# Phase tables by summed turns and one sine, and reciprocal roots as a power on GpSimd, in a two-block sequence kernel

## The chip, the cores and the metric

One core of one Trainium2 chip runs the whole program. The metric is the device time in microseconds of one execution; the kernel before was run three times.

## The reference

The input is one sequence of 256 tokens of width 1024 and a context of 256 tokens. The first block has two layers. Each normalizes tokens and context, multiplies by a wide input matrix, and feeds three branches: latent attention, multi-scale pooling and a gated linear attention (GLA) in four heads, run forwards and backwards. The branches are merged under gates and multiplied by an output matrix, and the result is normalized and added to the residual. The second block has a delta-rule recurrence (RWKV-7), a diagonal state-space branch (S5) with 32 groups of 64 states, a merge, and a convolutional feed-forward part. Cut to what the change touches:

```
def rmsnorm(x, g):
    y = x * lax.rsqrt(mean(x * x, -1) + 1e-6)
    return y * g

def s5_branch(u, a_re, a_im, ...):
    lam = complex(a_re, a_im);  dt = exp(log_step)[:, None]
    a_bar = exp(lam * dt)
    b_bar = ((a_bar - 1.0) / lam)[..., None] * complex(b_re, b_im)
    states = associative_scan(s5_combine, (a_bar at each token, bu))
    y = real(einsum('gcp,blgp->blgc', c, states)) + d * ug
```

The kernel runs the state-space recurrence with the real factor |a_bar| alone and turns the phases outside of it. For that it needs the cosine and the sine of t times the angle for all 256 tokens t and each of the 2048 states: 16 tables of 128 states by 512 columns (256 cosines, 256 sines).

## The kernel before

Activations lie transposed, features in the partitions and tokens in the columns. Weights come in units of 128x2048 as two tiles `raw` (seven buffers), issued on SyncE's queue (L409, L417). `split` (L419 to L428) cuts each into a high part `wh`, cast by ScalarE (L424), and a low part `wl`, subtracted by VectorE or GpSimd (L426); four buffers each. `mm3` (L441) runs three matmuls per weight tile. The order on each engine is made by a scheduler from the order in the program and the readiness of operands; an operation that stands late in the program can be placed early where its engine is free.

**Reciprocal roots.** Column sums of squares come out of TensorE as one column per 128 tokens (`token_sums`, L460), so a root is taken of a tile of 128x2, 128x4 or 128x16. `rsqrt` (L482 to L497) does it on VectorE: an integer guess (L488), then two refinement steps, nine instructions in one chain up to L496. `bcast` (L468) spreads the result over the partitions by transposes. `rstd` and `rstd_cols` (L471 to L480) serve the latent attention and the GLA heads. `boundary` (L540 to L567) serves the passage from one residual to the next normed input: a root `r` of the mean square of the branch output, four steps (L562 to L565) that make the mean square of the new residual from sums that are ready beforehand, a second root, and two broadcasts. `enter` (L657 to L668) then goes through the eight tiles of the residual: `update_x` adds the normed output on GpSimd (L649, L650) or on VectorE (L653, L654), and `build_h` (L634 to L640) makes the normed input. The updates on VectorE are held behind the second root (`issue_after(b.chain_end.ins)`).

**Phase tables.** `s5_prepare` (L1351 on) works out the angle in turns, splits t into 16 a + c and takes 32 sines and 32 cosines for each state (L1376 to L1389). Then each of 16 tables is made of them by the addition theorem on GpSimd: four products, a difference and a sum of 128x256 (L1443 to L1448), and a DMA on SyncE's queue writes it to DRAM (L1450). The tables are read back in the second block (L1568). This runs woven with the merge of the GLA branch in layer 0 (`weave(s5_prepare(b), 19, merge(2, ygla), 8)`), and for this stretch `lo_every` is set so that all weight splits go to VectorE:

```
        b.lo_every = 1 << 30
        weave(s5_prepare(b), 19, merge(2, ygla), 8)
        b.lo_every = 4
```

The merge takes a tanh of each gate (ScalarE, L939), a product (VectorE, L943) and a sum (VectorE, L947).

Of the kernel before, what the change touches and what calls it, by code (L numbers as in the profile page):

```python
# [10 lines left out]
F32 = mybir.dt.float32  # L11
# [3 lines left out]
AF = mybir.ActivationFunctionType  # L15
ALU = mybir.AluOpType
AX = mybir.AxisListType.X

P = 128
# [66 lines left out]
def _constants():  # L86
    c = Layout()
# [22 lines left out]
    sg[:64, 3], sg[64:, 3] = 0.0, 1 / TAU  # L110
    c.add("sgn", sg)
    c.add("iota", np.broadcast_to(np.concatenate([16.0 * np.arange(16), np.arange(16)]).astype(np.float32), (P, 32)))
    c.add("zero", np.zeros((P, 1), np.float32))
    c.add("one", np.ones((P, P), np.float32))
    c.add("mean", np.full((P, 1), 1.0 / D, np.float32))
    c.add("mean2", np.full((P, 1), 2.0 / D, np.float32))
    j = np.arange(P)
    masks = []
    i = j[:, None] // 64 * 64 + np.arange(64)
# [239 lines left out]
class B:  # L359
# [119 lines left out]
        n = self.token_sums(ps, 0, acc)  # L479
        return self.bcast(self.rstd_cols(ps[:, :n], n, dim), n, pool)  # L480

    def rsqrt(self, m, n):  # L482

        nc = self.nc
        r = self.sm.tile([P, 16], F32, tag="r", name="r")[:, :n]
        t = self.sm.tile([P, 16], F32, tag="t", name="t")[:, :n]
        u = self.sm.tile([P, 16], F32, tag="u", name="u")[:, :n]
        nc.vector.tensor_scalar(r.bitcast(I32), m.bitcast(I32), -0.5, 1597463007.0, ALU.mult, ALU.add)  # L488
        nc.vector.tensor_mul(t, r, r)
        nc.vector.tensor_mul(t, t, m)  # L490
        nc.vector.scalar_tensor_tensor(r, t, -3.0, r, ALU.add, ALU.mult)
        nc.vector.tensor_mul(t, r, r)  # L492
        nc.vector.tensor_mul(t, t, m)
        nc.vector.tensor_scalar(u, t, -0.375 / 32, 1.25 / 8, ALU.mult, ALU.add)  # L494
        nc.vector.tensor_mul(u, u, t)
        self.chain_end = nc.vector.scalar_tensor_tensor(r, u, -0.9375, r, ALU.add, ALU.mult)  # L496
        return r  # L497


# [144 lines left out]
def update_x(b, k, st, xs, s_, pr, rs, on_pool):  # L644

    nc = b.nc
    o_ = st["out"][k]
    if on_pool:
        nc.gpsimd.tensor_mul(o_.ap, o_.ap, rs.ap)  # L649
        nc.gpsimd.tensor_add(xs[s_][k], xs[s_][k], o_.ap)  # L650
    else:
        with b.tc.issue_after(b.chain_end.ins):
            nc.vector.tensor_mul(o_.ap, o_.ap, pr[:, 0:256])  # L653
            nc.vector.tensor_add(xs[s_][k], xs[s_][k], o_.ap)  # L654
    b.S.drop(o_)


# [13 lines left out]
def trunk(b, l, xs, st, A):  # L671

    nc, S = b.nc, b.S
# [21 lines left out]
    if st is None:  # L695
# [3 lines left out]
        for s_ in range(2):  # L699
            acc, t = S.cols(256), S.cols(256)  # L700
# [5 lines left out]
            S.drop(acc, t)  # L706
        A = b.sm.tile([P, 16], F32, tag="bA", name="bA")[:, :4]
        nc.vector.tensor_scalar(A, ps[:, :4], EPS, None, ALU.add)
        pr2 = b.bcast(b.rsqrt(A, 4), 4, b.pb)
    if st:  # L710
        first_units()
    shift, G = b.mod[l][0], b.mod[l][1]
# [11 lines left out]
    else:  # L724
        h, st = st
        xpart = enter(b, st, xs, 1, A[:, 2:4], lambda k: [t[:, XC] for t in h[k]], gain_, shift_, (0, 1, 3, 5, 7))
        A = next(xpart)
# [597 lines left out]
MAGIC = 12582912.0  # L1325
# [25 lines left out]
def s5_prepare(b):  # L1351
# [26 lines left out]
    nc.vector.tensor_sub(m, m, r)  # L1378
    nc.vector.tensor_tensor(r3, iob, fl.unsqueeze(2).broadcast_to((P, N, 32)), ALU.mult)
    nc.vector.tensor_add(m, m, r)  # L1380
    sn, cs = S.get(), S.get()
    for t, ph in ((sn, 0.0), (cs, 0.25)):
        if ph:
            nc.vector.tensor_scalar(m, m, ph, None, ALU.add)
        nc.vector.tensor_scalar(r, m, MAGIC, -MAGIC, ALU.add, ALU.add)
        nc.vector.tensor_sub(t, m, r)
    zero = b.after((sn, cs), 0.0)
    for t in (sn, cs):
        nc.scalar.activation(t, t, AF.Sin, bias=zero, scale=6.283184)  # L1389
    S.put(m, r)  # L1390
    yield
    sn3, cs3 = (t.rearrange("p (a c) -> p a c", c=32) for t in (sn, cs))

    s1, c1 = sn3[:, :, 17], cs3[:, :, 17]
    ur, ui, n2, kr, ki = sm("ur"), sm("ui"), sm("n2"), sm("kr"), sm("ki")
    nc.vector.tensor_mul(ur, rho, c1)
    nc.vector.tensor_scalar(ur, ur, -1.0, None, ALU.add)
# [34 lines left out]
        b.s5["w"].append(d)  # L1432
    S.put(cre, cren, cimn)
    yield
    ring = [(S.get(), S.get()) for _ in range(2)]
    for i in range(16):
        tab, tp = ring[i % 2]
        a3 = lambda t: t.rearrange("p (a c) -> p a c", c=16)
        can = cs[:, i * 32:i * 32 + 16].unsqueeze(2).broadcast_to((P, 16, 16))
        san = sn[:, i * 32:i * 32 + 16].unsqueeze(2).broadcast_to((P, 16, 16))  # L1440
        cbn = cs[:, i * 32 + 16:i * 32 + 32].unsqueeze(1).broadcast_to((P, 16, 16))
        sbn = sn[:, i * 32 + 16:i * 32 + 32].unsqueeze(1).broadcast_to((P, 16, 16))
        nc.gpsimd.tensor_tensor(a3(tab[:, 0:256]), can, cbn, ALU.mult)  # L1443
        nc.gpsimd.tensor_tensor(a3(tp[:, 0:256]), san, sbn, ALU.mult)
        nc.gpsimd.tensor_tensor(a3(tab[:, 256:512]), san, cbn, ALU.mult)
        nc.gpsimd.tensor_tensor(a3(tp[:, 256:512]), can, sbn, ALU.mult)
        nc.gpsimd.tensor_sub(tab[:, 0:256], tab[:, 0:256], tp[:, 0:256])
        nc.gpsimd.tensor_add(tab[:, 256:512], tab[:, 256:512], tp[:, 256:512])  # L1448
        d = b.tc.dram_tile([P, 512], F32, name=f"s5t{i}")
        nc.sync.dma_start(d, tab)  # L1450
        b.s5["tab"].append(d)
        yield
    S.put(sn, cs, *ring[0], *ring[1])


def second_block(b, xs, st, A):
# [172 lines left out]
    def rwkv_chain():  # L1629
# [29 lines left out]

        m16 = b.sm.tile([P, 16], F32, tag="m16", name="m16")  # L1660
        nc.vector.tensor_scalar(m16, nk[:, 0:16], 1e-24, None, ALU.max)
        rn = b.rsqrt(m16, 16)
        rnk = b.sm.tile([P, 16], F32, tag="rnk", name="rnk")
        nc.vector.tensor_copy(rnk, rn)
        yield
# [225 lines left out]
            S.drop(sq)  # L1891
        m16 = b.sm.tile([P, 16], F32, tag="m16", name="m16b")
        nc.vector.tensor_scalar(m16, nk[:, 0:16], 1.0 / 64, 64e-5, ALU.mult, ALU.add)
        rn = b.rsqrt(m16, 16)
        rnk = b.sm.tile([P, 16], F32, tag="rnk", name="rnk2")
        nc.vector.tensor_copy(rnk, rn)
        for q in range(4):
# [211 lines left out]
```

## Time and profile before

| | |
|---|---|
| median of 3 runs | 1556.37 us (1552.61 to 1558.96) |
| the profiled execution | 1556.99 us |
| its span, first to last instruction | 1555.2 us |
| mean granted TensorE clock | 0.954 |
| VectorE, ScalarE, GpSimd busy | 1101.0, 688.8, 491.1 us |

The span is the time between the first and the last instruction of the trace. Busy is the union of an engine's instructions. Idle time stands in front of the instruction that ended it, with what released it. Not every idle time costs something: only one on the engine that sets the end does.

### The profile page before, as it was taken

To read this page: it belongs to the slowest core of one execution; us is meant where nothing else is said; L and a number is where in the kernel's file an instruction comes from. 1 tells how busy PE (TensorE), PEld (TensorE's weight loads), DVE (VectorE), ACT (ScalarE), POOL (GpSimd) and SP (SyncE) were. 2 spreads that over 40 slices of the span, in tenths; PEclk is the share of its full clock that TensorE was granted. 3 is DMA by queue.
4 is the path that set the end of the run, shared out by engine and by line. 5 is a ranking of instruction groups with operands and counts; after the bars stand their busy time and mean duration, and the time that the engine had idled before them with its cause. 6 is when DMAs were issued, how large, how long until landed. Compare 5 with 4: busy or idle time off the path is not lost. (4 is left out here: it accounts for less than half of the span.)

```text
span 1555.2 us, 27544 instructions
## 1 busy us (share of the span) xinstructions
PE 1435.6 (92%) x10700; PEld 1216.2 (78%) x10700; DVE 1101.0 (71%) x2215; ACT 688.8 (44%) x1279; POOL 491.1 (32%) x503
## 2 busy tenths in 40 slices
PE   5999999998999999899998889979899999699996
PEld 1676776876788878886877789968668999699996
DVE  4565567887779555865579977768988549798843
ACT  3434445443433334454554455633532435376642
POOL 1000003354336954510035331334543003421212
PEclk8999999999999999899989999979999999799998
DMA  9534431321224253334024236734231325266560
GB/s 355 192 106 155 127 128 33 94 66 55 67 88 124 82 209 103 96 109 163 14 82 122 77 115 177 258 127 129 78 95 37 95 64 169 69 196 185 177 189 28
DMA packets 61043, 187.92 MB, mean 121 GB/s; under 512 B 7024, under 2 KB 8560, under 8 KB 60912
## 3 DMA queue, kind: packets, MB, share of 16 engines
q1 hardware_dynamic: 60912, 186.16, 38.2%
q8 instruction: 84, 1.38, 0.4%
q14 instruction: 47, 0.39, 0.1%
HBM read 180.10 MB, written 6.03 MB: 120 GB/s over the span
## 5 line engine op out<-in xcount | busy, mean ns | idle before, releaser
L424 ACT CAST wh<-raw 128x1024 fp32r<-128x1024 f32 (+1 forms) x296 | 279.5, 949 | 281.0 <-PE y L441 55.7
L426 DVE TENSOR_TENSOR wl<-raw,wh 128x1024 fp32r<-128x1024 f32 (+1 forms) x225 | 266.2, 1185 | 170.0 <-ACT wh L424 166.6
L426 POOL TENSOR_TENSOR wl<-raw,wh 128x1024 fp32r<-128x1024 f32 (+1 forms) x71 | 144.7, 2038 | 616.1 <-ACT wh L424 584.1
L441 PE MATMUL z_merge<-s,wh 128*128 128x512 f32 (+1 forms) x768 | 200.6, 351 | 1.8 <-ACT s L939 1.8
L441 PEld LDWEIGHTS z_merge<-s,wh 128*128 128x128 f32 x768 | 136.1, 198 | 19.7 <-ACT s L939 2.4
L441 PE MATMUL z_merge<-s,wl 128*128 128x512 f32 (+1 forms) x384 | 133.6, 348 | 0.3 <-DVE wl L426 0.2
L441 PE MATMUL pbr<-s,wh 128*128 128x256 f32 (+1 forms) x512 | 120.1, 326 | 0.8 <-DVE s L432 0.7
L441 PE MATMUL pup<-s,wh 128*128 128x256 f32 x656 | 118.5, 283 | 0.1
L441 PEld LDWEIGHTS pup<-s,wh 128*128 128x128 f32 x656 | 102.5, 192 | 0.2 <-ACT wh L424 0.2
L441 PE MATMUL y<-s,wh 128*128 128x256 f32 x496 | 98.1, 294 | 0.0
L441 PE MATMUL pwo<-s,wh 128*128 128x256 f32 (+1 forms) x448 | 94.1, 307 | 3.8 <-ACT s L1247 3.1
L441 PEld LDWEIGHTS pbr<-s,wh 128*128 128x128 f32 x512 | 86.8, 192 | 9.8 <-DVE s L432 1.0
L441 PE MATMUL pup<-s,wl 128*128 128x256 f32 x328 | 92.8, 283 | 0.0
L441 PEld LDWEIGHTS y<-s,wh 128*128 128x128 f32 x496 | 78.6, 193 | 7.8 <-issue 4.8
L441 PEld LDWEIGHTS z_merge<-s,wl 128*128 128x128 f32 x384 | 76.1, 198 | 9.5 <-DVE wl L426 1.1
L441 PE MATMUL pbr<-s,wl 128*128 128x256 f32 (+1 forms) x256 | 83.1, 325 | 0.0
L441 PEld LDWEIGHTS pwo<-s,wh 128*128 128x128 f32 x448 | 75.0, 199 | 7.7 <-ACT s L1247 3.7
L1134 ACT ACTIVATE s<-s 128x512 f32<-128x512 f32 (+1 forms) x64 | 33.2, 523 | 89.9 <-DVE s L1133 75.2
L441 PE MATMUL y<-s,wl 128*128 128x256 f32 x248 | 71.3, 287 | 0.0
L441 PE MATMUL pwo<-s,wl 128*128 128x256 f32 (+1 forms) x224 | 68.4, 306 | 1.5 <-DVE wl L426 1.5
L431 ACT CAST s<-s 128x256 fp32r<-128x256 f32 (+1 forms) x88 | 42.6, 488 | 60.7 <-DVE s L1204 17.9
L441 PE MATMUL pdn<-s,wh 128*128 128x256 f32 x352 | 63.4, 283 | 0.0
(480 smaller groups left out, 3618.8 us busy)
## 6 DMA issues: line engine op xcount, KB each, us to landing
raw<-wts SPq DMA_DIRECT2D x294, 512.0 KB, 4.4
s<-wts SPq DMA_DIRECT2D x57, 256.0 KB, 5.4
s5t<-s SPq DMA_DIRECT2D x16, 256.0 KB, 2.0
s<-s5t SPq DMA_DIRECT2D x16, 256.0 KB, 3.2
s<-xc SPq DMA_DIRECT2D x8, 256.0 KB, 5.0
x<-xc SPq DMA_DIRECT2D x8, 256.0 KB, 5.1
s<-tabs SPq DMA_DIRECT2D x4, 256.0 KB, 4.5
out<-s SPq DMA_DIRECT2D x8, 128.0 KB, 1.8
```

Of the source, the lines that this page charges most:

```text
L424: self.nc.scalar.copy(hi[:, :n], src)
L426: self.last_lo = eng.tensor_sub(lo[:, :n], src, hi[:, :n])
L431: self.nc.scalar.copy(hi, src)
L441: self.nc.tensor.matmul(ps, u, v[:, cols], start=start and n == 0, stop=stop and n == last)
L1134: nc.scalar.activation(E[:, lo:], E[:, lo:], AF.Exp, scale=1.0 / TAU)
```

## The change

The tables: the 32 small sines and cosines are no longer taken. VectorE adds the turns of 16 a and of c for all 256 tokens (once for the sine, once with a quarter turn more for the cosine), takes off the nearest whole number (two steps), and ScalarE takes one sine of the 512 columns. Four tables form a group: a helper (`after`, L445 on) waits for all four and hands a zero to the four sines, whose table set differs from that of the tanh. Of the small values only the step of one token is still needed (`s1`, `c1`).

The roots: `rsqrt` becomes a single power with exponent -0.5 on GpSimd, except for the first norm and the two 128x16 tiles, which keep the steps (`steps=True`). `chain_end` is now the power, so the hold moves from the updates on VectorE to those on GpSimd.

```
+    c.add("mhalf", np.full((P, 16), -0.5, np.float32))
...
-    def rsqrt(self, m, n):
+    def rsqrt(self, m, n, steps=False):
...
+        if not steps:
+            self.chain_end = nc.gpsimd.tensor_tensor(r, m, self.c("mhalf")[:, :n], ALU.pow)
+            return r
...
     if on_pool:
-        nc.gpsimd.tensor_mul(o_.ap, o_.ap, rs.ap)
-        nc.gpsimd.tensor_add(xs[s_][k], xs[s_][k], o_.ap)
+        with b.tc.issue_after(b.chain_end.ins):
+            nc.gpsimd.tensor_mul(o_.ap, o_.ap, rs.ap)
+            nc.gpsimd.tensor_add(xs[s_][k], xs[s_][k], o_.ap)
     else:
-        with b.tc.issue_after(b.chain_end.ins):
-            nc.vector.tensor_mul(o_.ap, o_.ap, pr[:, 0:256])
-            nc.vector.tensor_add(xs[s_][k], xs[s_][k], o_.ap)
+        nc.vector.tensor_mul(o_.ap, o_.ap, pr[:, 0:256])
+        nc.vector.tensor_add(xs[s_][k], xs[s_][k], o_.ap)
...
-    sn, cs = S.get(), S.get()
-    for t, ph in ((sn, 0.0), (cs, 0.25)):
-        if ph:
-            nc.vector.tensor_scalar(m, m, ph, None, ALU.add)
-        nc.vector.tensor_scalar(r, m, MAGIC, -MAGIC, ALU.add, ALU.add)
-        nc.vector.tensor_sub(t, m, r)
-    zero = b.after((sn, cs), 0.0)
-    for t in (sn, cs):
+    nc.vector.tensor_scalar(r, m, MAGIC, -MAGIC, ALU.add, ALU.add)
+    nc.vector.tensor_sub(m, m, r)
...
+    nc.vector.tensor_copy(s1, m3[:, :, 17])
+    nc.vector.tensor_scalar(c1, s1, 0.25, None, ALU.add)
+    nc.vector.tensor_scalar(k, c1, MAGIC, -MAGIC, ALU.add, ALU.add)
+    nc.vector.tensor_sub(c1, c1, k)
+    zero = b.after((s1, c1), 0.0)
+    for t in (s1, c1):
         nc.scalar.activation(t, t, AF.Sin, bias=zero, scale=6.283184)
...
+    nc.vector.tensor_copy(mc[:, 0:256].rearrange("p (i a) -> p i a", a=16), m3[:, :, 0:16])
+    nc.vector.tensor_scalar(mc[:, 256:512].rearrange("p (i a) -> p i a", a=16), m3[:, :, 0:16], 0.25, None, ALU.add)
+    rd = S.get()
     for i in range(16):
-        tab, tp = ring[i % 2]
...
-        nc.gpsimd.tensor_tensor(a3(tab[:, 0:256]), can, cbn, ALU.mult)
-        nc.gpsimd.tensor_tensor(a3(tp[:, 0:256]), san, sbn, ALU.mult)
-        nc.gpsimd.tensor_tensor(a3(tab[:, 256:512]), san, cbn, ALU.mult)
-        nc.gpsimd.tensor_tensor(a3(tp[:, 256:512]), can, sbn, ALU.mult)
-        nc.gpsimd.tensor_sub(tab[:, 0:256], tab[:, 0:256], tp[:, 0:256])
-        nc.gpsimd.tensor_add(tab[:, 256:512], tab[:, 256:512], tp[:, 256:512])
-        d = b.tc.dram_tile([P, 512], F32, name=f"s5t{i}")
-        nc.sync.dma_start(d, tab)
+        if i % 4 == 0:
+            tabs = [S.get() for _ in range(4)]
+        tab = tabs[i % 4]
+        t4 = tab.rearrange("p (e a c) -> p e a c", e=2, c=16)
+        for e in range(2):
+            am = mc[:, 256 * (1 - e) + 16 * i:256 * (1 - e) + 16 * i + 16].unsqueeze(2).broadcast_to((P, 16, 16))
+            bm = m3[:, i, 16:32].unsqueeze(1).broadcast_to((P, 16, 16))
+            nc.vector.tensor_tensor(t4[:, e], am, bm, ALU.add)
+        nc.vector.tensor_scalar(rd, tab, MAGIC, -MAGIC, ALU.add, ALU.add)
+        nc.vector.tensor_sub(tab, tab, rd)
+        if i % 4 == 3:
+            zero = b.after(tabs, 0.0)
+            for j, t in enumerate(tabs):
+                nc.scalar.activation(t, t, AF.Sin, bias=zero, scale=6.283184)
+                d = b.tc.dram_tile([P, 512], F32, name=f"s5t{i - 3 + j}")
+                nc.sync.dma_start(d, t)
```

## Rows read from the trace of the kernel before

**Rows 1.** The page's first part: busy us, share of the span, instructions.
```profile
PE 1435.6 (92%) x10700; PEld 1216.2 (78%) x10700; DVE 1101.0 (71%) x2215; ACT 688.8 (44%) x1279; POOL 491.1 (32%) x503
```
**Rows 2.** Stretches in the table stage: length, busy us per engine, clock, DMA share, GB/s.
```profile
474.00:500.00 26.00, 26.00 (x122) 21.65 (x121) 24.65 (x41) 9.35 (x13) 20.19 (x21) 1.00 0.48 143
500.00:570.00 70.00, 67.98 (x290) 54.85 (x289) 39.09 (x42) 20.57 (x31) 62.00 (x76) 0.98 0.32 99
```
**Rows 3.** GpSimd's groups by line: count, busy us, mean ns, idle before.
```profile
L1448 POOL TENSOR_TENSOR s<-s,s 128x256 f32<-128x256 f32 x16 | 16.5, 1031 | 0.0
...
L1443 POOL TENSOR_TENSOR s<-s 128x256 f32<-128x256 f32 x16 | 11.0, 688 | 8.4 <-DMA s5t<-s 7.5 <-ACT s L1389 0.9
```
**Rows 4.** SyncE's waits: us in total, times, longest.
```profile
SPq L1450 <- POOL s L1448: 64.6, 15, 6.2
```
**Rows 5.** ScalarE's time line: start, us, instruction, idle before and its releaser.
```profile
472.72 1.28 ACT L1389 ACT_TABLE_LOAD   x1
474.02 0.72 ACT L1389 ACTIVATE s<-s,after 128x512 f32<-128x512 f32 x1
...
481.39 1.28 ACT L939 ACT_TABLE_LOAD   x1
...
554.62 1.04 ACT L424 CAST wh<-raw 128x1024 fp32r<-128x1024 f32 x1 [7.33 <-DMA raw<-wts]
```
**Rows 6.** TensorE's time line in the table stage, the one stop.
```profile
556.22 0.73 PE L441 MATMUL z_merge<-s,wh 128*128 128x512 f32 x2 [1.77 <-ACT s L939]
```
**Rows 7.** VectorE's time line: undisturbed steps of the kinds that are added.
```profile
443.14 0.42 DVE L1133 TENSOR_TENSOR s<-s,s 128x256 f32<-128x256 f32 x1
...
467.08 0.43 DVE L1377 TENSOR_SCALAR s<-s 128x512 f32<-128x512 f32 x1
467.55 0.69 DVE L1378 TENSOR_TENSOR s<-s,s 128x512 f32<-128x512 f32 x1
```
**Rows 8.** VectorE's merge sums at 500 to 570 us, columns as in rows 3.
```profile
L947 DVE TENSOR_TENSOR s<-s,s 128x512 f32<-128x512 f32 x6 | 6.6, 1094 | 0.0
```
**Rows 9.** TensorE's time line: broadcasts of a root that came late.
```profile
97.81 0.65 PE L468 MATMUL ps_rb<-cons,r 128*128 128x128 f32 x4 [2.06 <-DVE r L496]
...
628.46 0.40 PE L468 MATMUL ps_rb<-cons,r 128*128 128x128 f32 x2 [2.78 <-DVE r L496]
...
682.84 0.65 PE L468 MATMUL ps_rb<-cons,r 128*128 128x128 f32 x4 [1.51 <-DVE r L496]
...
692.26 0.43 PE L468 MATMUL ps_rb<-cons,r 128*128 128x128 f32 x2 [0.97 <-DVE r L496]
...
1545.51 0.66 PE L468 MATMUL ps_rb<-cons,r 128*128 128x128 f32 x2 [2.12 <-DVE r L496]
```
**Rows 10.** The chain that ended last, at the boundary before the feed-forward part: start, us.
```profile
1337.49 0.07 DVE m L548
...
1339.91 0.16 DVE bs L561
...
1342.73 0.63 DVE r L491
...
1346.90 0.68 PE ps_rb L468 x2
...
1349.99 9.98 PE pen L441 x69
```
**Rows 11.** GpSimd's time line: a split near the early root; an update at the boundary.
```profile
93.05 2.41 POOL L426 TENSOR_TENSOR wl<-raw,wh 128x1024 fp32r<-128x1024 f32 x1 [17.26 <-DMA x<-xc]
...
1342.61 0.72 POOL L649 TENSOR_TENSOR s<-s 128x256 f32<-128x256 f32 x1 [9.11 <-ACT s L662]
```
**Rows 12.** GpSimd's narrowest products, by line and shape.
```profile
L978 POOL TENSOR_TENSOR s<-s,cons 128x8 f32<-128x8 f32 x2 | 0.5, 285 | 0.0
...
L978 POOL TENSOR_TENSOR s<-s,cons 128x1 f32<-128x1 f32 x2 | 0.3, 189 | 0.1
```
**Rows 13.** A stretch behind the boundary into the second block, columns as in rows 2.
```profile
1030.00:1036.00 6.00, 5.88 (x27) 5.59 (x28) 5.96 (x16) 1.85 (x6) 0.79 (x1) 0.51 0.00 0
```

More of the change, by code (lines that the diff above doesn't have):

```diff
@@ L495, in rsqrt @@
         nc.vector.tensor_mul(u, u, t)
-        self.chain_end = nc.vector.scalar_tensor_tensor(r, u, -0.9375, r, ALU.add, ALU.mult)
+        nc.vector.scalar_tensor_tensor(r, u, -0.9375, r, ALU.add, ALU.mult)
         return r
@@ L708, in trunk @@
         nc.vector.tensor_scalar(A, ps[:, :4], EPS, None, ALU.add)
-        pr2 = b.bcast(b.rsqrt(A, 4), 4, b.pb)
+        pr2 = b.bcast(b.rsqrt(A, 4, True), 4, b.pb)
     if st:
@@ L1380, in s5_prepare @@
     nc.vector.tensor_add(m, m, r)
-    sn, cs = S.get(), S.get()
-    for t, ph in ((sn, 0.0), (cs, 0.25)):
-        if ph:
-            nc.vector.tensor_scalar(m, m, ph, None, ALU.add)
-        nc.vector.tensor_scalar(r, m, MAGIC, -MAGIC, ALU.add, ALU.add)
-        nc.vector.tensor_sub(t, m, r)
-    zero = b.after((sn, cs), 0.0)
-    for t in (sn, cs):
+    nc.vector.tensor_scalar(r, m, MAGIC, -MAGIC, ALU.add, ALU.add)
+    nc.vector.tensor_sub(m, m, r)
+    S.put(r)
+    mc = S.get()
+    s1, c1 = sm("s1"), sm("c1")
+    nc.vector.tensor_copy(s1, m3[:, :, 17])
[4 more added lines that the diff above has]
+    for t in (s1, c1):
         nc.scalar.activation(t, t, AF.Sin, bias=zero, scale=6.283184)
-    S.put(m, r)
     yield
-    sn3, cs3 = (t.rearrange("p (a c) -> p a c", c=32) for t in (sn, cs))
-    s1, c1 = sn3[:, :, 17], cs3[:, :, 17]
     ur, ui, n2, kr, ki = sm("ur"), sm("ui"), sm("n2"), sm("kr"), sm("ki")
@@ L1434, in s5_prepare @@
     yield
-    ring = [(S.get(), S.get()) for _ in range(2)]
+    m3 = m.rearrange("p (a c) -> p a c", c=32)
+    nc.vector.tensor_copy(mc[:, 0:256].rearrange("p (i a) -> p i a", a=16), m3[:, :, 0:16])
+    nc.vector.tensor_scalar(mc[:, 256:512].rearrange("p (i a) -> p i a", a=16), m3[:, :, 0:16], 0.25, None, ALU.add)
+    rd = S.get()
     for i in range(16):
-        tab, tp = ring[i % 2]
[L1438 to L1442, printed above, removed]
-        nc.gpsimd.tensor_tensor(a3(tab[:, 0:256]), can, cbn, ALU.mult)
-        nc.gpsimd.tensor_tensor(a3(tp[:, 0:256]), san, sbn, ALU.mult)
-        nc.gpsimd.tensor_tensor(a3(tab[:, 256:512]), san, cbn, ALU.mult)
-        nc.gpsimd.tensor_tensor(a3(tp[:, 256:512]), can, sbn, ALU.mult)
-        nc.gpsimd.tensor_sub(tab[:, 0:256], tab[:, 0:256], tp[:, 0:256])
-        nc.gpsimd.tensor_add(tab[:, 256:512], tab[:, 256:512], tp[:, 256:512])
-        d = b.tc.dram_tile([P, 512], F32, name=f"s5t{i}")
-        nc.sync.dma_start(d, tab)
-        b.s5["tab"].append(d)
+        if i % 4 == 0:
[14 more added lines that the diff above has]
+                nc.sync.dma_start(d, t)
+                b.s5["tab"].append(d)
+            S.put(*tabs)
         yield
-    S.put(sn, cs, *ring[0], *ring[1])
+    S.put(m, mc, rd)
 def second_block(b, xs, st, A):
@@ L1661, in rwkv_chain @@
         nc.vector.tensor_scalar(m16, nk[:, 0:16], 1e-24, None, ALU.max)
-        rn = b.rsqrt(m16, 16)
+        rn = b.rsqrt(m16, 16, True)
         rnk = b.sm.tile([P, 16], F32, tag="rnk", name="rnk")
@@ L1893, in rwkv_chain @@
         nc.vector.tensor_scalar(m16, nk[:, 0:16], 1.0 / 64, 64e-5, ALU.mult, ALU.add)
-        rn = b.rsqrt(m16, 16)
+        rn = b.rsqrt(m16, 16, True)
         rnk = b.sm.tile([P, 16], F32, tag="rnk", name="rnk2")
```

## The prediction

> **What bounds the kernel now.** I read the page's busy times first: TensorE is busy for 1435.6 of 1555.2 us [rows 1]. What an edit on another engine can give back therefore lies in the 120 us in which TensorE stands still, and what it can cost lies where TensorE has no slack to give. So I then looked up both places that the change touches: the stretch in which the phase tables are made, by busy time in stretches, and every matmul that stood idle until a reciprocal root was ready, in the time lines and in the chain of waits.
>
> The table stretch is bound by TensorE: 26.00 busy of 26 us at 474 to 500, 67.98 of 70 at 500 to 570 [rows 2]. GpSimd is nearly full there (62.00 of 70) but sets no end itself; VectorE is full in the first part (24.65 of 26) and half empty after it (39.09 of 70). GpSimd reaches TensorE only through the DMA queue: SyncE waits 64.6 us in 15 waits for a finished table before it can issue what is queued behind, and that is weights [rows 4]. At 554.62 ScalarE has waited 7.33 us for such weights [rows 5], and TensorE stands 1.77 us for the tanh queued behind that cast [rows 6]. That is all the tables cost now.
>
> The roots are different: nine small VectorE steps one after another, and TensorE's broadcast behind them. TensorE waits 2.06, 2.78, 1.51, 0.97 and 2.12 us at five of them [rows 9]. At two boundaries (the one before the feed-forward part is shown, the one before the second block at 1018 to 1030 us repeats it) the chain of waits itself runs through them [rows 10].
>
> **The change, part by part: the tables.** Removed: 16 times six GpSimd products and sums, 0.69 to 1.03 us each (first and last of the six lines shown [rows 3]), some 83 us of GpSimd that nothing but SyncE waits for. Added per table on VectorE: two broadcast sums of 128x256 at 0.42, one rounding of 128x512 at 0.43, one difference of 128x512 at 0.69 [rows 7], so 1.96 us; 16 tables are 31.4 us, and the four helpers that hand a zero to ScalarE (five narrow steps of 0.16 each [rows 10]) 3.2 more: 34.6 us. Taken away from VectorE: one rounding, one difference and a shift of 512 columns (1.5 us), and the stretching of its own operations by GpSimd. In 500 to 570 us a merge sum takes 1.09 us [rows 8] where the same shape takes 0.69 undisturbed [rows 7]; with the shapes' undisturbed durations throughout its 39.09 us shrink to about 32. VectorE then has 32 + 34.6 = 66.6 of these 70 us to do, or spreads it to 610. It fits, barely. The cover is that the weight splits stand earlier in the program than the tables they compete with, so a table step can delay a split by its own 0.69 us at most. If that cover is gone, VectorE paces TensorE.
>
> Added on ScalarE: 16 sines of 0.72 us for two, and four times a switch to the sine's table and back, 1.28 us each way [rows 5]: 14 x 0.72 + (8 - 2) x 1.28 = 17.8 us more. It has room (20.57 busy of 70 us [rows 2]), but it comes in blocks of 4 x 0.72 + 2 x 1.28 = 5.4 us, in which the casts and tanh queued behind wait. A wait of 7.33 us on the same queue cost TensorE 1.77 us [rows 5, 6]. The 16 table writes on SyncE's queue stay, now in bursts of four behind a block; the weights queued behind them wait for ScalarE instead of GpSimd.
> On the table load the rows are plain: the sine starts at 474.02, right when the load of 472.72 ends [rows 5], so 1.28 us is the whole price. The Trainium skill (ScalarE: Activation LUTs, What ACT_TABLE_LOAD costs) speaks against the change here: it counts about 1283 ns for the load and about 1380 ns more for a drain. By that rule a block would be 8.2 us; the trace agrees with the load and shows no drain.
> Net of this part: best +3.5 us gained (the 1.77 us stop goes, and with it the 3.4 us at half clock behind it, the 0.98 of [rows 2], worth 1.7); worst four blocks that each cost the 1.77 us stop and 1.7 us of clock, 14 us lost. I take 1.8 us lost: one block in four uncovered, since the present 7.3 us waits also show as a stop only once.
>
> **The roots.** Of 24 chains 21 become one GpSimd power. The trace has no power. Its nearest rows are GpSimd's narrow products: 0.189 us for one column, 0.285 for eight [rows 12]; that is the low end. The high end is the chain it replaces: nine steps of 0.19 us, 1.74 us. I take c = 0.6 us, about twice the 0.285 row. Site by site:
> - The full boundary [rows 10]. The mean is ready at 1337.56. The first root now takes until 1341.3, because VectorE's queue holds, amid the chain, a step that waits for TensorE's next sums (1339.91). On GpSimd the root is ready at 1338.2, before those sums. The four steps to the new mean then end at 1340.9 instead of 1342.1, and the second root at 1340.9 + c. Before it took 4.6 us, its last six steps 0.63 to 0.66 us each [rows 10], because GpSimd was updating x beside it. The broadcast pair then ends at 1341.7 + c instead of 1347.57. But the x updates on GpSimd now queue behind the second power, and the first tile of the normed x needs three of them at 0.72 us [rows 11]: 1343.1 + c against 1347.6. So the gain is 4.5 - c, 4.0 us with rounding. Two such boundaries: 8.0 us. VectorE's own x updates lose their hold and can go in the wait; that is free.
> - The context boundary at 628.46: the 2.78 us stop is the second root's, again stretched by the x updates; the power would be done near 622, the stop goes: 2.8 us.
> - 682.84 and 692.26: 1.51 and 0.97 us [rows 9]; there the chain is interleaved with weight splits, and one power is out of that queue: 2.5 us.
> - 97.81: 2.06 us [rows 9]. GpSimd is in a 2.41 us split from 93.05 [rows 11]; if the power queues behind it, it is done at 96.1 against 97.75. I count 0.9, half of the 1.7 us, since the gated-attention stage behind it has stops of its own that may take it up.
> - The last root: 1.74 - 0.6 = 1.1 us, straight off the end.
> - The eight in the gated-attention heads and the two at 647 to 653 end no idle time of TensorE: matmuls of other branches hide them, so nothing gained. Each puts c into GpSimd's queue ahead of products that TensorE does wait for; 4.8 us of queue in all, taken at nothing because 8 x 9 VectorE steps leave the other queue of the same stage. If that cover is gone, it costs up to these 4.8 us.
> The sum is 8.0 + 2.8 + 2.5 + 0.9 + 1.1 = 15.3 us; at c = 0.19 it is 16.9, at c = 1.74 about 11. Less 1.8 for the tables: 13.5 us.
> The first power may have a price of its own that no row here shows. The Trainium skill (GPSIMD Engine Reference, Instruction dispatch) says that the first call into freshly loaded code pays about 6 us. By it the first root, at 80.65 us, would be some 4 us late once, and the sum an estimated 9.5 us.
>
> **From the profile to the forecast.** The profiled execution lasted 1556.99 us, 1.8 us more than its span and 0.6 more than the median of 1556.37. 1556.4 - 13.5 is 1543 us.
>
> **Rivals.**
> *The table stretch becomes the bound.* For it: VectorE has 66.6 of 70 us to do, ScalarE stops for 5.4 us four times, and TensorE has shown that one stop of that kind reaches it [rows 5, 6]. Against: the present waits of 7.3 us reach it once only. Four exposed blocks cost 14 us instead of 1.8: 1555 us, between 1549 and 1562.
> *The power is dear, and it ends slower.* The place is GpSimd's queue at the boundaries, the price c. At c above 2.3 us the first power is later than the sums that hide it, and each boundary loses 2 us for each us of c; setting all sites to zero, the point from which the change loses is c near 3.5 us. At 6 us both boundaries lose 5 us each, the end 4, the sites at 93 to 98 and 622 to 692 some 8, and the heads a few more: about 1574 us. For it: GpSimd's own arithmetic is slow (0.69 to 1.03 us for 128x256 steps where VectorE takes 0.42 [rows 3, 7]), and a power is no single step. Against: with two or four columns there is little to compute, and the narrow products of [rows 12] cost 0.2 to 0.3 us.
> *More is given back.* After each boundary TensorE runs at half clock: at 1030 to 1036 it is busy 5.88 of 6 us with a granted clock of 0.51 [rows 13], the lower level of 1.2 GHz; a similar stretch of 10 us follows the context boundary. If shorter stops leave the clock up, 3 us at one and 5 at the other come on top: 1534 us.
> That the change doesn't do what it says would be the power placed behind a GpSimd split at each site; with 2.4 us a split this is the dear power at c = 3, the upper end of the forecast's neighbours, and I count it there.
>
> **How the numbers follow.** Forecast (1536 to 1548): 0.55. Table stretch: 0.22. Dear power: 0.13. More given back: 0.10. Half a per cent, 7.8 us, is about what a measurement of this kernel can tell from no change. The forecast and the last rival are faster by more than that: 0.65. The table rival lies mostly within it (0.18), the rest of it and the dear power mostly above: 0.20 same, 0.15 slower. The range for 8 in 10 reaches from 1532 into both slower rivals, to 1558.
>
> **What would show it.** Right: each power near 0.6 us on GpSimd; the broadcast at both boundaries 5 us nearer to the mean; the first normed x tile paced by GpSimd's updates; no stops before the broadcasts at the sites of [rows 9]; VectorE near 90% and ScalarE with eight table loads in the table stretch, and TensorE still full. Wrong: a power over 2 us; TensorE stops in 490 to 570 that end on a cast, a tanh or a split; more than eight table loads there; or a table stretch that runs on past 610 us.

## The result and the profile after

| | before | after |
|---|---|---|
| median of 4 runs | 1557.45 us (1552.61 to 1558.96) | 1538.94 us (1536.60 to 1543.70) |
| ratio | | 0.989, 95% interval 0.9855 to 0.9926 |
| the profiled execution, its span | 1556.99, 1555.2 us | 1536.71, 1534.9 us |
| mean granted TensorE clock | 0.954 | 0.960 |

The change makes the kernel 18.5 us faster, where 13.5 was forecast. The page's first part and the same two stretches of the table stage (columns as in [rows 2]), of the kernel after:

```profile
PE 1427.4 (93%) x10700; PEld 1212.0 (79%) x10700; DVE 1070.7 (70%) x2113; ACT 713.5 (46%) x1307; POOL 433.8 (28%) x428
...
474.00:500.00 26.00, 26.00 (x119) 21.48 (x118) 25.49 (x58) 8.93 (x12) 3.84 (x2) 1.00 0.40 126
500.00:570.00 70.00, 67.95 (x292) 55.56 (x291) 50.80 (x99) 47.63 (x61) 0.00 (x0) 0.98 0.52 169
```

GpSimd is empty from 500 to 570 us (62.00 before [rows 2]); VectorE has 50.80, not the 66.6 of the forecast: its 32 table sums lie between 470.0 and 521.6, part of them ahead of 500; TensorE is as full as before.

**A balance by landmarks.** To see where the time went, I paired every matmul of one trace with the same matmul of the other (same tile written, same place in the sequence) and took the difference of their start times. The difference stays flat for hundreds of microseconds and jumps at a few places; the jumps add up to the whole. Three traces are compared with the kernel before: the changed kernel, and two experiments below that make one half of the change each. Positive is gained, in us:

| stretch | forecast | changed kernel | tables alone | roots alone |
|---|---|---|---|---|
| start to 65 us (no edit there) | 0 | -0.6 | 0.3 | -3.1 |
| roots at 81 and 98 us | 0.9 | -0.6 | 0.0 | -2.0 |
| gated-attention heads, first layer | 0 | 2.9 | 0.6 | 1.3 |
| table stretch, 474 to 605 us | -1.8 | 2.5 | 6.7 | -0.8 |
| context passage and behind it, to 660 | 2.8 | 5.4 | 0.0 | 5.3 |
| latent attention, 682 and 692 us | 2.5 | 3.2 | 0.0 | 3.0 |
| rest of the second layer | 0 | 1.5 | 1.3 | 1.6 |
| passage into the second block | 4.0 | 1.7 | 0.5 | 1.5 |
| state-space part | 0 | 0.6 | 1.6 | 0.7 |
| passage into the feed-forward part | 4.0 | 2.4 | 0.3 | 2.7 |
| last root | 1.1 | 1.3 | -0.3 | 1.3 |
| sum | 13.5 | 20.3 | 11.0 | 11.5 |

The first line shows how far two executions differ where nothing is changed: up to 3 us, nearly all of it before 38 us. Lines without an edit differ by up to 1.6 us (the state-space part with the tables alone), and the heads by more, as shown below, so a line is read from a jump that its trace explains, not from its size alone. The total came out near the forecast, but two terms were mis-sized in opposite directions, the table stretch (4.3 us more than forecast) and the two full passages (3.9 less). The heads, the context passage and the rest of the second layer, 7.0 us above their forecasts together, make up most of the surplus.

### The profile page after: what moved, and what is told of

It reads as the page before. It is cut to its first block, busy times and chain, and to the rows that moved or that the text cites. A ratio compares the mean times of both kernels' runs of the same rounds, so it can differ in the third digit from the quotient of the medians.

```text
span 1534.9 us, 27423 instructions
## 1 busy us (share of the span) xinstructions
PE 1427.4 (93%) x10700; PEld 1212.0 (79%) x10700; DVE 1070.7 (70%) x2113; ACT 713.5 (46%) x1307; POOL 433.8 (28%) x428
## 3 DMA queue, kind: packets, MB, share of 16 engines
q8 instruction: 84, 1.38, 0.4%
## 5 line engine op out<-in xcount | busy, mean ns | idle before, releaser
L427 DVE TENSOR_TENSOR wl<-raw,wh 128x1024 fp32r<-128x1024 f32 (+1 forms) x225 | 263.1, 1170 | 163.9 <-ACT wh L425 160.9
L432 ACT CAST s<-s 128x256 fp32r<-128x256 f32 (+1 forms) x88 | 42.6, 487 | 57.1 <-DVE s L1208 14.3
```

The lines of the kernel that those rows point to most:

```text
L427: self.last_lo = eng.tensor_sub(lo[:, :n], src, hi[:, :n])
L432: self.nc.scalar.copy(hi, src)
```

## The experiments

All ratios are to the kernel before on the same chip.

**Tables alone, roots alone.** The first undoes the roots, the second the tables:

```
# e1                                   # e2: the kernel before, and
-        if not steps:                 +        if not steps:
+        if False:                     +            self.chain_end = nc.gpsimd.tensor_tensor(r, m, ..., ALU.pow)
+ hold on VectorE's updates, as before + hold on GpSimd's updates, as after
```

> Only the tables are changed; all 24 roots are the nine VectorE steps, and the hold of the updates is that of the kernel before. The sum of the prediction says 1.8 us slower than the kernel before (1.5 to 2.5 slower). Against it stands the balance of the two traces: matmul by matmul the changed kernel gains from 1.67 us at 500 us to 4.21 us at 600 us, so the tables should be worth 2.5 us (faster). A third theory is that part of what comes later, 4.2 to 9.6 us between 610 and 635 us, also belongs to the tables, since GpSimd is free and its products at the context boundary come early: then this run is 4 to 7 us faster.

> Only the roots and the hold are changed; the tables are products on GpSimd as before. The prediction's sum for the roots is 15.3 us faster with powers of 0.6 us; with the measured powers (0.82 us for two columns, 1.44 on average for four) its own formula gives about 13. The balance of the two traces leaves 20.3 - 2.5 = 17.8 us for the roots if the parts add. If the parts do not add, because the powers and updates now stand behind nothing that the table products once filled, this run and the tables alone fall short of the 18.5 us of the whole by 3 us or more.

Measured: 1545.22 us, ratio 0.9941 (0.9921 to 0.9961), for the tables; 1544.73 us, 0.9939 (0.9920 to 0.9957), for the roots. So 9.7 and 10.2 us: the tables are worth as much as the roots, and my sign for them was wrong; the two halves add up to 19.9 us, the whole to 18.5, no difference that these intervals could tell. The tables' gain is not at the context boundary, as the third theory had it, but in the table stretch itself: TensorE has no stop left there.

```profile
500.00:570.00 70.00, 70.00 (x311) 57.80 (x310) 52.55 (x103) 47.23 (x63) 0.00 (x0) 1.00 0.52 173
```

That is the stretch of [rows 2] with the tables alone: 70.00 of 70 us against 67.98. What is gone are two stops of the kernel before: that of [rows 6], worth 4.6 us by the balance, and a second at 581.41, worth 2.1, which the prediction did not have. The queue of SyncE behind which the first one arose, and what stood in front of the second, all of the kernel before:

```profile
541.49 8.97 SPq L1450 DMA_DIRECT2D s5t<-s  x3
550.55 0.38 SPq L409 DMA_DIRECT2D raw<-wts  x1
...
577.76 2.39 POOL L426 TENSOR_TENSOR wl<-raw,wh 128x1024 fp32r<-128x1024 f32 x1 [12.35 <-ACT wh L424]
578.15 2.55 DVE L947 TENSOR_TENSOR s<-s,s 128x512 f32<-128x512 f32 x1
581.41 0.49 PE L441 MATMUL pwo<-s,wh 128*128 128x512 f32 x1 [1.33 <-ACT s L1247]
```

A weight unit is issued at 550.55, only after three table writes that waited 8.97 us for GpSimd's products; the cast of 554.62 [rows 5] is waiting for that unit. The second stop has another last link. The ScalarE operation in front of it (L1247, at 580.73) waits for a merge sum of VectorE that took 2.55 us instead of 0.69 [rows 7], beside a weight split on GpSimd that began 0.39 us ahead of it. With the tables alone the same sum began at 570.75, 0.21 us ahead of that split; it took 0.69 us, and there is no stop. Casts had waited 4.44, 1.26 and 0.70 us for weights at 565 to 573 in the kernel before; that the sum met the split because of these late weights is likely, but not shown.

**The table writes on GpSimd's queue.** The kernel before, with one line changed, to tell the queue from the products themselves:

```
-        nc.sync.dma_start(d, tab)
+        nc.gpsimd.dma_start(d, tab)
```

> The kernel before, in which only the 16 table writes go from SyncE's queue to GpSimd's own; every product stays where it was. With the tables alone as VectorE sums and sines TensorE lost its stops at 554 and 580 us, 4.6 and 2.1 us. Theory: both come from the weights that stand behind the table writes in SyncE's queue (a cast waits 7.33 us, then 4.44, while SyncE waits 8.97 us for products). Then this kernel loses both stops too, and is 6 to 7 us faster than the kernel before, about 1549 us. Rival: they come from GpSimd itself, which stretches VectorE's merge sums to 1.09 us (0.69 undisturbed) and so the merge; then the stops stay, and the time is that of the kernel before within 1.5 us.

Measured: 1564.84 us, ratio 1.0061 (1.0037 to 1.0084): 7.8 us slower, which neither theory gave. The two stops are gone, and the balance shows the 4.5 and 2.1 us regained between 555 and 582 us, but 18 us are lost ahead of that, at 513 to 531. Two of TensorE's four stops there, and what VectorE and GpSimd do:

```profile
526.73 0.79 PE L441 MATMUL pbr<-s,wh 128*128 128x512 f32 x1 [7.66 <-ACT s L431]
530.91 0.80 PE L441 MATMUL pbr<-s,wh 128*128 128x512 f32 x1 [3.38 <-DVE s L432]
...
514.53 3.57 DVE L432 TENSOR_TENSOR s<-s,s 128x512 fp32r<-128x512 f32 x1 [0.68 <-ACT s L431]
518.02 4.33 DVE L426 TENSOR_TENSOR wl<-raw,wh 128x512 fp32r<-128x512 f32 x1
526.71 4.14 DVE L432 TENSOR_TENSOR s<-s,s 128x512 fp32r<-128x512 f32 x1 [0.68 <-ACT s L431]
...
517.50 0.58 POOL L1450 DMA_DIRECT2D s5t<-s  x1
521.75 0.58 POOL L1450 DMA_DIRECT2D s5t<-s  x1
530.26 0.58 POOL L1450 DMA_DIRECT2D s5t<-s  x1
```

VectorE's subtractions of 128x512, 0.68 us undisturbed, take 3.57 to 4.33 us, and each ends within 0.03 us of the end of a GpSimd DMA issue (518.10 and 518.08, 522.35 and 522.33, 530.85 and 530.84): the products that GpSimd runs back to back between two issues keep VectorE out. A cast of ScalarE waits 10.55 us for VectorE (at 526.06), and TensorE for the cast; the four stops are 14.9 of the 18 us. So in this run GpSimd's products had a price through VectorE. For the queue the run is weaker than it looks: with TensorE 18 us late, the weights had more time to arrive anyway. The queue's rows above carry that reading for the first stop; the run only does not contradict it. The second stop is absent here as with the tables alone: the merge sum began at 591.82, the split at 591.98, and the sum took 0.69 us.

**The passages by steps, and each power doubled.**

```
# e3                                    # e4
-        r = self.rsqrt(m, n)           +            r2 = self.sm.tile(...)
+        r = self.rsqrt(m, n, True)     +            nc.gpsimd.tensor_tensor(r2, m, ..., ALU.pow)
...                                                  self.chain_end = nc.gpsimd.tensor_tensor(r, m, ..., ALU.pow)
```

> The changed kernel, with the roots of the boundaries (three passages and the last root) as VectorE steps again and the hold as before; the roots of the latent attention and of the heads stay powers. By the prediction these sites are worth 8.0 + 2.8 + 1.1 = 11.9 us, so this run is 11.9 us slower than the changed kernel, about 1551 us. By the balance of the traces the two boundaries gave 1.7 and 2.4 us only, the last root 1.25, and the context boundary 4 to 5.4: 9.4 to 10.8 us. If the boundaries were worth little and the gain sits in the latent attention's roots, it is under 7 us slower.

> The changed kernel with every power issued twice, the first into a tile that nobody reads: the price of a power is doubled at each site, by 0.82 us for two columns and 1.0 to 1.4 for four. By the prediction's reading each us on the power costs each boundary 2 us, the other exposed sites 1 us each and the heads nothing: 3.3 at the two boundaries, 1.6 at the context boundary, 0.8 at the end, 1.0 to 1.4 each at 81, 95, 672 and 682 us: 9 to 11 us slower than the changed kernel. If the heads' sites count too (8 powers, 1 us each), it is 16 to 19 slower. If TensorE's waits at the boundaries end on something else (GpSimd's updates are behind the power, so this would not help; the sums are), under 6.

Measured: 1546.46 us, ratio 0.9947 (0.9927 to 0.9968), with the passages by steps; 1550.07 us, 0.9970 (0.9956 to 0.9984), with each power doubled. Set against the changed kernel's median the one is 7.5 us slower, against its gain over the kernel before 10.0; the other 11.1 or 13.6. So the passages and the last root carry 7.5 to 10 us, less than the 11.9 of the prediction's sum, and doubling the 21 powers costs somewhat more than the 9 to 11 that I counted. By the balance against the changed kernel the surplus is at the context passage, not in the heads: 5.9 us are lost between 605 and 660, where I had counted 1.6, and over the same 146 matmuls there, from 615 to 640 in the changed kernel, the granted clock is 0.76 instead of 0.86. The heads lose 2.2 us, against 4.1 between the fastest and the slowest of the kernels with single powers there (below), so a price of the heads' powers is not shown.

**Which step of the passage fails.** In the changed kernel the step that makes the mean starts at 1320.91 (the chain counts it from 1320.99, when VectorE is free for it), the first matmul of the feed-forward part at 1329.99. The chain of waits in between:

```profile
1320.99 0.08 DVE m L552
...
1321.13 0.89 POOL r L488
...
1322.07 0.69 PE ps_rb L469 x2
1322.75 1.51 PE ps_ss L461 x8
...
1324.29 0.17 DVE bs L565
...
1324.55 0.16 DVE bt L566
1324.71 0.33 DVE s L657
1325.05 0.07 DVE bt L567
1325.12 0.33 DVE s L657
1325.44 0.07 DVE bt L568
1325.52 0.34 DVE x L658
1325.85 0.08 DVE bA L569
...
1326.00 0.81 POOL r L488
1326.81 1.50 POOL s L654 x2
1328.31 1.37 POOL x L655 x2
```

Three things stand in it that I had not counted or had called free: the second sums wait on TensorE behind the broadcast of the first power; VectorE's updates of x (L657, L658) go between the four steps of the mean; and GpSimd does two products before its first sum, so the first tile of x is ready 2.2 us after the second power. Three runs take them one at a time.

```
# e6, in boundary: bcast moved behind token_sums(ps, n, last[2], ...)
# e7, in update_x:  +  with b.tc.issue_after(b.mean_end.ins):   (VectorE's branch)
# e8, at both full passages:  (0, 1, 3, 5, 7)  becomes  (1, 3, 5, 7)
```

> The changed kernel, with the second sums of squares issued on TensorE ahead of the broadcast of the first root (at the three passages). Theory: TensorE takes its instructions in order, so the sums that the new mean needs stand behind the first power; with the order turned they are done at 1323.3 instead of 1324.3 us, and the passage before the feed-forward part (mean at 1320.91 to the first matmul at 1329.99 in the changed kernel: 9.1 us) takes 8.1; 2 us in all over two passages and about 1 at the context. Rival: the four steps wait for the power itself, then the passage stays at 9.1.

> The changed kernel, with VectorE's updates of x held behind the new mean. Theory: freed from their hold they go between the four steps of the mean, which now start 0.40 us apart (0.20 before), so the passage before the feed-forward part (9.1 us from the mean to the first matmul) becomes 8.4, and the kernel 1 to 2 us faster over three passages. Rival, that of the prediction: the updates fill time in which VectorE waits anyway, the passage stays at 9.1 or gets longer by the updates that now come later (0.8 us).

> The changed kernel, with the first tile of x updated on VectorE instead of GpSimd at the two full passages (as it is at the context). Theory of the prediction: the first normed tile is paced by GpSimd's updates behind the second power (1326.8 to 1329.0 us in the changed kernel), while its broadcast is there at 1327.6; then the passage before the feed-forward part takes 7.7 us instead of 9.1, and the kernel is 2 to 3 us faster. Rival: VectorE, with one tile more, is late with the tiles behind the first, TensorE stops there instead, and the kernel gains less than 1 us.

Measured, with the passage read from the traces (from the start of the step that makes the mean, as every line of this table):

| | time, ratio (95%) | new mean done | first matmul |
|---|---|---|---|
| before | | 4.70 | 11.24 |
| changed kernel | 1538.94, 0.9890 (0.9855 to 0.9926) | 5.02 | 9.09 |
| sums first | 1537.17, 0.9874 (0.9853 to 0.9895) | 5.03 | 9.10 |
| updates behind the mean | 1539.64, 0.9886 (0.9868 to 0.9903) | 4.40 | 8.35 |
| first tile on VectorE | 1538.00, 0.9879 (0.9857 to 0.9901) | 5.02 | 7.66 |

No time differs from that of the changed kernel by more than the intervals; the passages do. The hold gives 0.74 us, as its theory had it. The first tile gives 1.43, but a new stop of 0.80 us stands behind it, so 0.6 is left:

```profile
1331.58 1.01 PE L442 MATMUL pen<-s,wh 128*128 128x256 f32 x3 [1.01 <-ACT s L640]
1333.60 0.58 PE L442 MATMUL pen<-s,wh 128*128 128x256 f32 x1 [0.80 <-DVE s L641]
```

The first of the three says nothing: the order on TensorE stayed that of the changed kernel, as the broadcast still came 1.16 us after the mean, ahead of the sums. A later place in the program didn't move it; in a run below it is held there.

**The narrow roots outside of the passages.** First the latent attention and the heads by steps, then the heads alone:

```
# e5, in rstd_cols                        # e12, in the heads
-        return self.rsqrt(m, n)          -            r = b.rstd_cols(ps[:, :n], n, P)
+        return self.rsqrt(m, n, True)    +            r = b.rstd_cols(ps[:, :n], n, P, steps=True)
```

> The changed kernel with the roots of the latent attention and of the gated-attention heads as VectorE steps again; powers stay at the boundaries and at the end, all of two columns. These roots are the dear ones (1.0 to 2.0 us for four columns against 1.74 for the steps). By the prediction they are worth 0.9 + 2.5 + 0 us. With the tables alone TensorE had no stop before the gating cast at 511 us, with the powers of the heads it has one of 1.82 us, worth 4.1 with the half clock behind it. If these powers are what moves the cast behind two blocks of sines, the stop goes, and the run is at 1538.9 + 3.4 - 4.1, about 1538 us. If the stop has another cause, it stays, and the run is 3 to 5 us slower than the changed kernel, about 1543.

> The changed kernel with the eight roots of the gated-attention heads as VectorE steps; the powers of the latent attention and of the boundaries stay. The stop of 1.82 us before the gating cast at 511 us was absent with both these and the latent attention's roots as steps. Theory: the head's power at 474 us moves the order of the sines against the gating cast, so the stop is absent here too, and with the latent attention's stops gone as well (0.7 at 672, none at 682 us) the run is 2 to 4 us faster than the changed kernel, about 1536. Rival: the power of the latent attention at 81 us shifts the whole plan, the stop stays, and the heads' powers are worth 0 to 3 us by themselves: 1539 to 1542.

Measured: 1537.64 us, ratio 0.9873 (0.9852 to 0.9895), and 1540.94 us, 0.9909 (0.9888 to 0.9930). All these powers together change nothing that can be measured. With the heads by steps the stop at 511 us is gone in both, which is worth 4 us, but in the second run the heads themselves take 5.1 us more than in the changed kernel, between 86 and 408 us.

About 2 us of that are the price of the steps, judged by one trace of each kernel. Over the same matmuls, from 105 to 440 us in the kernel before, the seven kernels with steps in the heads took 332.3 to 337.5 us, 334.7 on average, and the six with single powers there 329.8 to 333.9, 332.5 on average. Two things recur. A stop at 326 us is 2.28 us long with steps and 1.72 to 1.76 with powers. And behind a stop of 3.15 us at 390, the same in all within 0.05 us, 36 matmuls took 5.13 us at a granted clock of 1.00 in the changed kernel, and 6.87 us at 0.75 in the run with the heads by steps; all seven kernels with steps and one of the six with powers are slow there, and why is open. The other 3 us are the clock behind two more stops, at 270 and 402 us, where it differs between kernels with equal heads too: the 26 matmuls behind the first took 4.37 us at 0.66 in the changed kernel, and 3.00 us at 1.00 in the run with the passages by steps.

The stop at 511 us is set by how the planner lays the sines among ScalarE's other work. All six kernels with the new tables and the heads' powers have it (1.82 to 1.84 us), and none of the five with the new tables and the heads by steps. ScalarE in the changed kernel, and the stop:

```profile
504.79 1.28 ACT L1459 ACT_TABLE_LOAD   x1
506.08 1.34 ACT L1459 ACTIVATE s<-s,after 128x512 f32<-128x512 f32 x2
507.44 1.28 ACT L896 ACT_TABLE_LOAD   x1
508.73 0.60 ACT L896 ACTIVATE s<-z_gla_gate 128x512 f32<-128x512 f32 x1
509.23 0.61 ACT L425 CAST wh<-raw 128x512 fp32r<-128x512 f32 x1
509.86 1.28 ACT L1459 ACT_TABLE_LOAD   x1
511.15 1.33 ACT L1459 ACTIVATE s<-s,after 128x512 f32<-128x512 f32 x2
512.39 0.60 ACT L432 CAST s<-s 128x512 fp32r<-128x512 f32 x1
...
513.05 0.50 PE L442 MATMUL pbr<-s,wh 128*128 128x512 f32 x1 [1.82 <-ACT s L432]
```

The gate's tanh (L896) and the cast of the gated product (L432) each stand behind two sines and a table load. With the heads by steps one sine, and neither a second one nor a weight cast, stands between the tanh and the cast, which starts 2.55 us after the tanh instead of 3.66; the tanh itself starts 1.71 us ahead of TensorE's run of `pbr` matmuls instead of 0.29. TensorE doesn't wait. ScalarE there:

```profile
515.89 0.60 ACT L896 ACTIVATE s<-z_gla_gate 128x512 f32<-128x512 f32 x1
516.51 1.28 ACT L1459 ACT_TABLE_LOAD   x1
517.81 0.73 ACT L1459 ACTIVATE s<-s,after 128x512 f32<-128x512 f32 x1
518.44 0.60 ACT L432 CAST s<-s 128x512 fp32r<-128x512 f32 x1
```

**What the runs point to, together.** The sums held on TensorE ahead of the first broadcast, the updates behind the mean, the first tile on VectorE, steps for the heads and for the first layer's latent attention; and the same with GpSimd updating tiles 2, 4 and 6.

```
+        with self.tc.issue_after(self.sum_end.ins):
+            pr = self.bcast(r, n, self.pa)
...
+        with b.tc.issue_after(b.mean_end.ins):
             nc.vector.tensor_mul(o_.ap, o_.ap, pr[:, 0:256])
```

> The changed kernel with what the runs so far point to: TensorE's second sums held ahead of the broadcast of the first root, VectorE's updates of x behind the new mean, the first tile updated on VectorE; the heads' roots and those of the first layer's latent attention as VectorE steps, powers at the boundaries, the end and the second layer's latent attention. The passage before the feed-forward part (9.09 us from the mean to the first matmul in the changed kernel) had 8.35 with the hold and 7.66 with the first tile on VectorE. If these add, and the sums ahead give the 0.9 us that they stand behind the power, it takes 6.0 to 6.9 us, two of them save 4.4 to 6.2, and without the gating cast's stop at 511 us (absent where the heads take steps) 1 to 3 us more: 1531 to 1535 us. If shorter passages only turn into stops behind the first tiles (0.80 us was seen), about 1536 to 1538.

> As the run with the mended orders, but GpSimd updates tiles 2, 4 and 6 of x at the two full passages (as at the context) instead of 1, 3, 5 and 7. The stop of 0.80 us behind the first tile, seen with the first tile on VectorE, ends on VectorE's subtraction for tile 1, whose update is on GpSimd. If that update is late, this arrangement removes the stop, 0.8 us twice, and the kernel is 1 to 2 us faster than the run with the mended orders. If VectorE's own work on five tiles is the limit, the stop moves to the tiles after it, and the times are equal within 1 us.

Measured: 1530.92 us, ratio 0.9842 (0.9817 to 0.9868), and 1529.12 us, 0.9830 (0.9803 to 0.9857): 26 and 28 us faster than the kernel before. The passage takes 6.44 and 6.27 us instead of 9.09, and the stop at 511 us is absent. In the second the stop behind the first tile (0.88 us in the first) is gone, but the times cannot tell the two apart. The chain of the first one, for comparison with the one above:

```profile
1314.73 0.07 DVE m L552
...
1315.25 1.88 PE ps_ss L461 x8
...
1318.20 0.17 DVE bA L571
...
1318.44 0.70 POOL r L488
```

From the mean at 1314.73 to the new mean at 1318.37 it is 3.6 us: no power stands in that part any more, only the sums, as the forecast had assumed for the changed kernel.

## Why the prediction was right, and where it was not

**Right in sign and within the range** (1538.94 in 1532 to 1558), 4 us below the value. That rests partly on two errors that cancel, and so partly on luck: the tables have the wrong sign, and the full passages gave half. Two sums of the prediction do not come out of their own terms either. A gain of 3.5 for the stop that goes, less 3.5 for one uncovered block, is 0 and not 1.8 lost. The losses listed for a power of 6 us add up to 22 us and more, so 1578 us and not 1574.

*The tables.* The failed step is the sentence "That is all the tables cost now". I took one stop, 1.77 us, as the whole present cost and 3.5 us as the most that could come back. The stop and what follows it were worth 4.6, and a second stop, 1.33 us at 581.41, behind a merge sum that a GpSimd weight split had stretched, 2.1 more. The charge against it, one uncovered block, came true: the stop at 511 us cost 4.1 us in the balance where I had 3.5 (1.77 and 1.7 for the clock). So the net is +2.5 and not -1.8, and with the sines laid well, as in the run with the tables alone, 6.7. The VectorE steps cost what they were said to (0.41, 0.42 and 0.69 us), and VectorE did not become the bound. ScalarE loaded the sine's table six times and the other back six times, twelve loads instead of the eight that I had named as the limit: the planner cut the groups of four into pieces. Beyond the stop at 511 us TensorE has none in the table stretch, as ScalarE had the room.

On the table load the Trainium skill's rule (ScalarE: Activation LUTs, What ACT_TABLE_LOAD costs) did not hold here: at 504.79 the load takes 1.28 us and the sine starts at 506.08; there is no further 1.38 us of drain.

*The powers.* By shape, of the kernel after (columns as in [rows 3]), then the first two in time order, with the weight split on VectorE that runs beside the first:

```profile
L488 POOL TENSOR_TENSOR r<-m,cons 128x4 f32<-128x4 f32 x7 | 10.1, 1442 | 55.2 <-DVE m L474 31.9 <-DVE ex_p L1345 12.2 <-ACT s L1090 11.0
L488 POOL TENSOR_TENSOR r<-m,cons 128x2 f32<-128x2 f32 x10 | 8.2, 824 | 39.8 <-DVE m L552 19.2 <-DVE m L474 9.9 <-DVE bs L565 6.1
L488 POOL TENSOR_TENSOR r<-bA,cons 128x2 f32<-128x2 f32 x4 | 3.2, 811 | 13.5 <-DVE bA L569 13.5
...
81.20 1.23 DVE L427 TENSOR_TENSOR wl<-raw,wh 128x1024 fp32r<-128x1024 f32 x1
81.33 1.97 POOL L488 TENSOR_TENSOR r<-m,cons 128x4 f32<-128x4 f32 x1 [4.94 <-DVE m L474]
95.54 1.01 POOL L488 TENSOR_TENSOR r<-m,cons 128x4 f32<-128x4 f32 x1 [12.23 <-DVE ex_p L1345]
```

I took 0.6 us within 0.19 to 1.74: two columns cost 0.82, four 1.44 on average, the nine steps 1.74. The averages hold waiting. The power at 81.33 began while a VectorE split was under way until 82.43, and took 1.97 us; that at 95.54 had no such neighbour, and took 1.01. It is not the price of being first: at 665.36 a later power of four columns, begun within another split, took 1.94, and in the run with each power doubled the second of the first pair took 1.01. Undisturbed, two columns take 0.70 us (673.57). So for two columns 0.6 was near the power's own time; the term that I left out is what VectorE does beside it. At 81 us, a site that I had not listed, it made a new stop of 1.73 us; at 98 us the stop fell from 2.06 to 0.76.

The first power began 0.08 us after its input was ready. The 6 us that the Trainium skill (GPSIMD Engine Reference, Instruction dispatch) gives for a first call into freshly loaded code are not there.

*The two full passages.* 1.7 and 2.4 us instead of 4.0 each. The failed steps are "before those sums" (the sums stood behind the power on TensorE; the new mean came 5.02 us after the old one, not 3.3), and "that is free" for VectorE's updates (0.74 us). That the first normed tile is paced by GpSimd's updates was right: moving it gave 1.43 us. With all three mended the passage is 4.8 us shorter than before; 0.88 of that goes to the stop behind the first tile, and by the balance the two passages then give 3.9 and 3.6 us, near the 4.0 of the forecast.

*The context passage.* 5.4 us instead of 2.8. The failed step is "the stop goes": the stop of 2.78 us [rows 9] gave way to stops of 2.82 us at 628, for VectorE's squares in front of the next sums, and of 1.14 us at 634, for a weight split. The gain is the clock. The same 356 matmuls before and after:

```profile
600.00:660.00 60.00, 53.07 (x356) 51.24 (x355) 43.38 (x113) 22.15 (x50) 29.29 (x33) 0.83 0.26 76
...
595.80:650.40 54.60, 47.54 (x356) 46.27 (x355) 37.20 (x80) 21.89 (x50) 32.03 (x37) 0.91 0.27 83
```

TensorE stands still for 7.1 us of the stretch, 6.9 before; the granted clock is 0.91 instead of 0.83, with less of the stretch at 1.2 GHz. This is the third rival, "more is given back", at one of its two places and in part (2.6 us of its 5), though not by its way, as the stops did not get shorter; why the clock stayed up is open. Behind the full passages it stays low as before.

*The latent attention and the last root* (3.2 for 2.5, 1.3 for 1.1) came out near their forecasts; at the first, stops of 2.48 us became one of 0.71, and the rest is the clock. *The heads* "end no idle time of TensorE", I said, so nothing gained; the stops bear that out but for 0.5 us. The zero was too small all the same: over all kernels the powers in the first layer's heads are worth about 2 us, that 0.5 and 1.6 by the granted clock behind another stop. The 2.9 us that the changed kernel gained, and the 5.1 that the run by steps lost on it, hold clock behind further stops, which differs as much between kernels with equal heads.

## What to carry over

A wait on the DMA queue is priced by everything that is queued behind it: follow each write that waits for an engine to the loads behind it, list every stop of the stretch and not only the largest, and ask what the engine that made the data does to its neighbours. A root that is ready sooner helps only as far as the next thing in line: look in the chain of waits for what then comes late on the in-order engines, here the sums behind a broadcast, the updates between four small steps, and the updates behind the power. A replacement of nine narrow steps by one operation should be weighed by shape and by what the neighbouring engine does at that moment: the power took 0.70 and 1.01 us undisturbed, and up to 1.97 beside VectorE's splits. At the passages, with two columns, it was worth it; in the first layer's heads, with four, it gave about 2 us, which a new stop elsewhere took back. And a stretch that gains without shorter stops should be read by its granted clock before the gain is put down to an edit.

## What was not expected of the hardware

GpSimd's power takes 0.70 us for 128x2 and 1.01 for 128x4 where no VectorE operation on two large SBUF tiles is under way when it begins, and up to 1.97 where one is. A VectorE step of the same width is 0.16 us.

VectorE's subtraction of two tiles can be kept out for a whole run of GpSimd products, not for one of them: 3.57 to 4.33 us against single products of 0.62 to 0.71, until a DMA issue came up in GpSimd's queue. The Trainium skill (SBUF — State Buffer, SBUF: two separate sides) says that whichever of the two starts first has the shared port for the whole instruction. The end of the subtraction fits: its last 0.6 us fall on the DMA issue, right behind the end of a product. But four or five products ended before that without VectorE getting its turn. In the kernel before, with GpSimd as busy (39.32 of 40 us at 500 to 540, against 38.93), the same subtractions took 0.69 to 1.21 us from 507 to 516, and it was GpSimd's products that were stretched, to 1.06 to 1.72 us for several of them; why VectorE got its turn there is open.
